# A hybrid decoder layer on one core: the FFN up-projection by Strassen's products, and the stages behind the retention issued in program order

## The chip, the core and the metric

One core of a Trainium2 chip runs the whole layer. The time of a run is the device time of that core in microseconds (us), from the program's start to its end; a profiled execution also gives its span (first to last recorded instruction) and the times of every instruction. TensorE (PE) multiplies, VectorE (DVE), ScalarE (ACT) and GpSimd (POOL) do the elementwise work, and the DMA engines move data between DRAM and the on-chip memory (SBUF). Matrix products land in PSUM.

## The reference, cut to what matters

Sequence of 16 meta tokens and 1024 tokens, width 1024, float32. The change touches what follows the retention: its output projection, the output projection of the differential attention, the gated merge with `w_out`, and the gated MLP.

```python
ro = (jax.nn.silu(rg) * ro) @ w_ret_o            # 4 heads x 512 -> 1024
do = do @ w_diff_o                               # 1024 -> 1024
mix = (sigmoid(g_ret) * ro + sigmoid(g_diff) * do) @ w_out
h = h + mix
u = rmsnorm(h, norm2_w)
up = causal_dwconv(u @ w_up, conv_w, conv_b)     # w_up: 1024 -> 2 x 2816, three taps
a, b = jnp.split(up, 2, axis=-1)
h = h + (jax.nn.silu(a) * b) @ w_down            # 2816 -> 1024
```

## The kernel before

Everything lies with channels on the 128 partitions and tokens along the free axis, 1040 tokens in three groups `QG` of 342, 342 and 342 columns (1026 of them are used behind the attention). Every float32 operand is split into a rounded high part and the rest, and a product is three matmuls, high by high, high by low, low by high (`bulk`, line 175 is the one place where they are recorded). A block of weights is 128 output channels by 1024 input channels, eight 128x128 tiles: `load_w` brings it in two halves of 128x512, ACT casts the high part (L227, tile `wh`), POOL subtracts for the low part (L230, tile `wl`). `next_w` keeps one block ahead.

The order on each engine comes from a scheduler that runs ahead over the whole program, bound by the buffers of the pools. Behind the retention come:

- `ret_out(h)`, the retention's output blocks, woven between the chunks of the next head; that of the last head stands alone at the end of `phase2`.
- `phase3`: the heads of the attention are reloaded and scaled (L986), eight output blocks of `w_diff_o` (three groups, 72 matmuls each), the gates from spilled tiles (sigmoid L996, multiplied on POOL L1006), the merge (L1012, L1013), its split (L242, L247), eight blocks of `w_out`, and the residual with its squares (L1034, L1040, L1041).
- `normed(m)`: the residual is scaled by the norm's weight and split (L250, L253); the sum of squares gives the reciprocal root `rb2` by a chain of some ten DVE operations (`rsqrt`, L273 to L293), and it is multiplied into the product only behind the matmul, where the up-projection leaves PSUM (L1094).
- `phase4`: for each of 22 f, two blocks of `w_up` (f and 22+f), 2 x 72 matmuls of 342 columns; each is scaled (L1094), convolved (`conv`, three DVE operations of 1024 columns, L1101 and L1103), silu on ACT (L1139), the product (L1140), its split by ACT (L242) and POOL (L247). Every two f, `down` adds 8 x 2 x 6 matmuls of 512 columns to the residual (L1118).

Of the kernel before, what the change touches and what calls it, by code (L numbers as in the profile page):

```python
# [97 lines left out]
class Builder:  # L98
    ATT_WEIGHT, RET_WEIGHT = 38.666666666666664, 27.0

    def __init__(self, ctx, tc, a, chunk_dec):
# [211 lines left out]
    def setup(self):  # L313
# [7 lines left out]
        pc = cp.tile([P, a["cols"].shape[1]], F32, name="cols")  # L321
# [7 lines left out]
    def constants(self):  # L329
# [8 lines left out]
        cr = cp.tile([P, nr], F32R, name="constsr")  # L338
# [405 lines left out]
    def phase1(self):  # L744
# [17 lines left out]
        order = []  # L762
        for n in range(0, NF, 2):
            down = [a["w_down"][n - 2], a["w_down"][n - 1]] if n else []
            up = [a["w_up"][f] for f in (n, NF + n, n + 1, NF + n + 1)]
            order += up[:2] + down + up[2:] if n < NF - 2 else up + down
        order += [a["w_down"][NF - 2], a["w_down"][NF - 1]]
# [193 lines left out]
    def phase2(self, rest, nrest):  # L961
# [12 lines left out]

    def phase3(self):
        V, A, G, S = self.V, self.A, self.G, self.S
        q = slice(HALO, T)
        dh, dl = [], []
        for h in range(DH):
            sp, sy = self.spill["do", h]  # L980
            d, y = self.big(), self.big()
            S.dma_start(out=d[:, q], in_=sp[:, q])
            for p, n in enumerate((258, 256, 256, 256)):
                t0 = HALO if p == 0 else NMETA + 256 * p
                S.dma_start(out=y[:, t0:t0 + n], in_=sy[p:p + 1, :n].to_broadcast([P, n]))
# [219 lines left out]
```

## Time and profile before

| | |
|---|---|
| three runs | 2597.95, 2599.13, 2600.05 us, median 2599.13 |
| profiled execution | 2597.52 us, its span 2595.7 us |
| PE busy | 97% of the span |
| DVE, ACT, POOL busy | 61%, 35%, 33% |
| PE's granted clock, mean | 0.99 |

The profiled execution is 1.8 us longer than its span; the difference lies around the span. A busy share is an average over the whole span. Matmul starts are recorded; one matmul's end overlaps the start of the next, so what a matmul costs is read from start to start.

### The profile page before, as it was taken

How to read it: one execution, taken by the hardware profiler on the slowest of the kernel's cores; microseconds unless marked ns; L12 is line 12 of the kernel's file. 1: busy time of each engine (PE TensorE's matmuls, PEld its weight loads, DVE VectorE, ACT ScalarE, POOL GpSimd, SP SyncE). 2: the span in 40 equal slices, each digit the busy share in tenths (PEclk: the TensorE clock that was granted, in tenths of full speed). 3: DMA queues.
4: the chain of work that ended last, by engine and by line, in shares of the span. 5: the costliest groups of instructions: out<-in, count | busy, mean ns of one | idle time of the engine just before them, and what ended most of it. 6: DMA issues, size and time to landing. Idle time of an engine off the chain costs nothing.

```text
span 2595.7 us, 40469 instructions
## 1 busy us (share of the span) xinstructions
PE 2518.1 (97%) x15444; PEld 2420.7 (93%) x15444; DVE 1575.6 (61%) x3239; ACT 899.0 (35%) x1879; POOL 852.7 (33%) x668
## 2 busy tenths in 40 slices
PE   7899999999999999999999998999999999999999
PEld 6888999999999999999999898999999999999998
DVE  8676756556473646453777888352466555555555
ACT  3244434344342434243456654332311111111111
POOL 4433343223132222212333332444333333332332
PEclk8999999999999999999999999999999999999999
DMA  4423141424233141423443434523111111111112
GB/s 176 103 70 101 54 130 62 125 82 117 81 81 102 61 117 58 125 84 109 112 107 89 114 91 130 167 94 110 46 49 45 45 49 49 48 43 49 49 49 85
DMA packets 171538, 224.55 MB, mean 87 GB/s; under 512 B 26712, under 2 KB 109264, under 8 KB 171344
## 3 DMA queue, kind: packets, MB, share of 16 engines
q1 hardware_dynamic: 165440, 202.70, 25.7%
q0 software_dynamic: 5760, 19.17, 3.6%
q8 instruction: 121, 1.98, 0.3%
q14 instruction: 73, 0.60, 0.1%
q10 hardware_dynamic: 144, 0.10, 0.0%
HBM read 160.20 MB, written 42.35 MB: 78 GB/s over the span
## 4 chain that ended last, share of the span: by engine, by line
PE 82%; DVE 9%; issue 4%; ACT 2%; DMA 2%; POOL 1%; SPq 1%; DVEq 0%; POOLq 0%; ACTq 0%
PE acc L175 47%; PE sc L175 27%; PE ot L175 3%; PE st L175 1%; PE sc L640 1%; DVE b L499 1%; ACT b L624 1%; DVE b L501 1%; DVE sh L498 1%; DVE b L617 1%; DVE b L247 1%; DMA b<-d 1%; DVE b L253 1%; DVE sql L247 1%; POOL wl L230 1%
## 5 line engine op out<-in xcount | busy, mean ns | idle before, releaser
L175 PE MATMUL acc<-b,wh 128*128 128x342 f32 (+3 forms) x6076 | 1485.0, 327 | 31.3 <-ACT wh L227 7.2
L175 PEld LDWEIGHTS acc<-b,wh 128*128 128x128 f32 x6076 | 1055.4, 190 | 46.5 <-ACT wh L227 7.1
L175 PE MATMUL acc<-b,wl 128*128 128x342 f32 (+3 forms) x3038 | 986.8, 325 | 0.8 <-POOL wl L230 0.8
L230 POOL TENSOR_TENSOR wl<-wr,wh 128x512 fp32r<-128x512 f32 x370 | 516.3, 1414 | 1081.3 <-ACT wh L227 1067.7
L175 PE MATMUL sc<-b,wh 128*128 128x342 f32 (+2 forms) x2452 | 616.9, 335 | 0.0
L175 PEld LDWEIGHTS acc<-b,wl 128*128 128x128 f32 x3038 | 576.4, 190 | 6.6 <-POOL wl L230 1.4
L175 PEld LDWEIGHTS sc<-b,wh 128*128 128x128 f32 x2452 | 432.7, 189 | 19.9
L227 ACT CAST wh<-wr 128x512 fp32r<-128x512 f32 x370 | 215.0, 618 | 583.8 <-issue 297.3
L175 PE MATMUL sc<-b,wl 128*128 128x342 f32 (+2 forms) x1226 | 409.7, 334 | 0.8 <-POOL wl L230 0.8
L247 POOL TENSOR_TENSOR b<-b,b 128x512 fp32r<-128x512 f32 (+2 forms) x90 | 147.3, 1637 | 317.5 <-ACT b L242 294.1
L175 PEld LDWEIGHTS sc<-b,wl 128*128 128x128 f32 x1226 | 231.7, 189 | 11.3 <-POOL wl L230 1.3
L242 ACT CAST b<-b 128x512 fp32r<-128x512 f32 (+2 forms) x135 | 100.1, 745 | 235.0 <-DVE b L1140 146.1
L624 ACT ACTIVATE b<-b,sm 128x272 f32<-128x272 f32 (+7 forms) x128 | 100.9, 788 | 187.7 <-DVE sm L623 159.7
L534 DVE TENSOR_TENSOR ev<-acc,b 128x342 f32<-128x342 f32 (+1 forms) x144 | 74.1, 515 | 151.1 <-PE acc L175 133.6
L1103 DVE SCALAR_TENSOR_TENSOR b<-b,cols,b 128x1024 f32<-128x1024 f32 x88 | 148.4, 1686 | 2.3
L617 DVE CUSTOM_DVE_ANT_0 b<-sc,consts 128x144 f32<-128x144 f32 (+6 forms) x224 | 106.0, 503 | 54.7 <-PE sc L175 54.6
L1094 DVE TENSOR_TENSOR b<-sc,b 128x342 f32<-128x342 f32 x84 | 42.5, 511 | 138.6 <-PE sc L175 138.6
L1118 DVE TENSOR_TENSOR b<-b,sc 128x512 f32<-128x512 f32 x117 | 78.6, 682 | 47.6 <-PE sc L175 47.6
L247 DVE TENSOR_TENSOR al<-sc,ah 128x512 fp32r<-128x512 f32 (+2 forms) x144 | 77.4, 539 | 47.0 <-ACT ah L242 44.9
L242 ACT CAST ah<-sc 128x512 fp32r<-128x512 f32 (+2 forms) x144 | 67.2, 468 | 110.4 <-PE sc L640 84.4
L500 POOL TENSOR_TENSOR sh<-sh,b 128x346 f32<-128x346 f32 (+1 forms) x48 | 48.9, 1019 | 143.2 <-DVE sh L498 120.5
L175 PE MATMUL sc<-b,b 128*128 128x264 f32 (+9 forms) x480 | 91.1, 310 | 1.4 <-DVE sm L617 1.4
(233 smaller groups left out, 2740.7 us busy)
## 6 DMA issues: line engine op xcount, KB each, us to landing
wr<-w_in SPq DMA_DIRECT2D x176, 256.0 KB
wr<-w_up SPq DMA_DIRECT2D x88, 256.0 KB
d<-ev SPq DMA_DIRECT2D x120, 171.0 KB
b<-b POOLq DMA_DIRECT2D x72, 260.0 KB, 4.3
b<-d SPq DMA_DIRECT2D x256, 64.0 KB
b<-d SPq DMA_DIRECT2D x24, 513.0 KB
wr<-w_down SPq DMA_DIRECT2D x44, 256.0 KB
b<-d SPq DMA_DIRECT2D x32, 260.0 KB
```

Of the source, the lines that this page charges most:

```text
L175: self.E.matmul(out, lhsT=l, rhs=r, start=start, stop=stop)
L227: self.A.copy(h, raw)
L230: self.G.tensor_sub(l, raw, h.bitcast(F32))
L242: self.A.copy(dh, src)
L247: (self.V if el == "V" else self.G).tensor_sub(dl, src, dh.bitcast(F32))
L500: G.tensor_mul(sh[:, :n], sh[:, :n], self.Sn[:, cs])
L534: V.tensor_mul(o[:, :n], ps[:, :n], self.rb[:, cs])
L617: V.tensor_tensor_reduce(out=sc_[:m, a0:a0 + sz], in0=ps[:m, :sz], in1=mk, scale=1.0, scalar=3e38, op0=ALU.add, op1=ALU.min, accum_out=sm[ ...
L624: A.activation(sc_[:m, :n], sc_[:m, :n], AF.Exp, bias=mx, scale=-1.0, accum_out=sm[:m, 10 + c:11 + c])
L1094: self.V.tensor_mul(up[:, t0:t0 + n], ps[:, :n], self.rb2[:, t0:t0 + n])
L1103: V.scalar_tensor_tensor(out=o[:, q], in0=up[:, NMETA - 2 + i:T - 2 + i], scalar=self.cw(i, fi), in1=o[:, q], op0=ALU.mult, op1=ALU.add)
L1118: self.V.tensor_add(h, h, ps)
```

## The change

The up-projection is cut into quarters: rows of `w_up` into lower and upper input channels (4 tiles each), its columns into the block of f and that of 22+f, the tokens into two halves of 516. The four quarter results come from seven products of quarter size (Strassen's algorithm in Winograd's form, called A, B, E, F, G, H, D), each 4 tiles x 3 matmuls x 2 pieces of 258 columns. Seven sums of token halves (`operand_a` to `operand_h`) are made once, seven weights for each f: two by DMAs that add while they write (`quad_sums`, on POOL's queue), two by POOL additions (S and T in `weights`), and all seven are split by ACT and POOL (`split_w`). The results are combined where they leave PSUM, the tap sums run in `act_steps` between the products of the next f, and every f's result goes to DRAM. `down` runs behind the last f and reloads them. The norm is now multiplied into the tokens before the products (`scaled`), so that sums can be formed.

`w_out` runs in two token halves, so its weights are loaded and split twice, and the norm of the first half runs in the second. From `back` on, the order on each engine is the program's own. `back` closes the pools of the first stages and opens new ones: `w2` with 128x512 quarters, PSUM as three double banks and two single ones. The last head's blocks 4 to 7 of `ret_out` move into `phase3`. The stages before are as they were, but for eight small memsets.

```diff
+        self.flush()
+        self.front.close()
...
+        self.wp = pool("w2", 11)
+        self.ps = pool("ps2", 3, space=PSUM)
+        self.queue = [a["w_ret_o"][14], a["w_ret_o"][15]] + [a["w_diff_o"][i] for i in range(8)] + 2 * [a["w_out"][i] for i in range(8)]
...
+        for i in (4, 2, 0):
+            self.coming.append(raws[i:i + 2])
+            self.fetch(self.queue.pop(0), raws[i:i + 2])
+        self.ready.append([self.split_w(r) for r in self.coming.pop(0)])
...
+    def split_w(self, raw):
+        w = self.quarter()
+        self.A.copy(w[0], raw)
+        self.G.tensor_sub(w[1], raw, w[0].bitcast(F32))
+        return w
...
+    def block(self, level=1):
+        w = self.ready.pop(0)
+        while len(self.ready) < level and self.coming:
+            self.arrive()
+            self.request()
+        return lambda k: tuple(t[:, k % 4, :] for t in w[k // 4])
...
+    def dbl(self): return self.ps.tile([P, 1024], F32, tag="d", name=self.nm("d"), bufs=3)
+    def sng(self): return self.ps.tile([P, 512], F32, tag="s", name=self.nm("s"), bufs=2)
...
+    HALF = [[(12, 256), (268, 256)], [(524, 258), (782, 258)]]
+    PIECES = [(0, 258), (258, 258)]
...
+        self.heads, self.wq, self.raws = [], {}, {}
+        nxt = self.normed_head(0)
+        for m in range(4, 8):
+            if m % 2 == 0:
+                w = self.block(m // 2 - 1)
+            outs, reads = self.triple()
+            self.product(outs, [(w(4 * (m % 2) + e), (self.gh[3][e], self.gl[3][e])) for e in range(4)])
+            for cs, p in reads:
+                V.tensor_add(self.like(self.racc[m], cs), self.like(self.racc[m], cs), p)
+            nxt()
+            nxt = self.normed_head(m - 3)
...
+            self.split(mh[m][:, 12:], ml[m][:, 12:], mx[:, 12:], el="G" if m % 2 and m < 7 else "V")
...
+        def finish(m, i, ps):
+            t0, n = self.HALF[i][0]
+            o = self.two(self.h[m][:, t0:t0 + 2 * n])
+            V.tensor_add(o, o, self.pair(ps, n))
+            hs = slice(8 + 516 * i, 524 + 516 * i)
+            S.dma_start(out=self.hs[m][:, 516 * i:516 * i + 516], in_=self.h[m][:, hs])
...
+                (V if i else G).tensor_add(sq[:, hs], sq[:, hs], x)
...
+            while m < 8:
+                w = self.block(2 - i)
+                ps = self.dbl()
...
+                finish(m, i, ps)
+                if i:
+                    if m == 0:
+                        squares(0)
+                    elif m == 1:
+                        stat()
+                    elif m == 2:
+                        spread(0)
+                    elif m < 7:
+                        for k in (2 * (m - 3), 2 * (m - 3) + 1):
+                            self.operand_a(k)
+                    if 3 <= m < 6:
+                        self.pre_weights(m - 3)
+                    if 2 <= m < 5:
+                        self.pre_loads(m - 2)
+                    elif m == 5:
+                        self.quad_loads(0)
+                    elif m == 6:
+                        self.quad_sums(0)
+                m += 1
+        squares(1)
+        self.weights(0, "SE")
+        self.quad_loads(1)
+        self.pro = {}
+        self.first_t(0)
+        self.first_t(1)
+        self.quad_sums(1)
+        stat()
+        self.first_t(2)
+        self.weights(0, "F")
+        self.first_b(0)
+        spread(1)
+        self.weights(1, "SE")
+        self.first_b(1)
+        self.first_b(2)
...
+    def scaled(self, k, i):
+        x = self.h[k][:, 8 + 516 * i:524 + 516 * i]
+        self.V.scalar_tensor_tensor(out=x, in0=x, scalar=self.n2[k], in1=self.rb2[:, 8 + 516 * i:524 + 516 * i], op0=ALU.mult, op1=ALU.mult)
...
+    def operand_a(self, k):
+        self.put("A" if k < 4 else "B", k % 4, self.scaled(k, 0))
...
+    def operand_e(self):
+        for k in range(4):
+            self.scaled(k, 1)
+            self.V.tensor_sub(self.half(k, 0), self.half(k, 0), self.half(k, 1))
+            self.put("E", k, self.half(k, 0), "G" if k % 2 else "V")
...
+    def operand_f(self):
+        for k in range(4):
+            self.scaled(4 + k, 1)
...
+    def operand_h(self):
+        for k in range(4):
+            self.V.tensor_sub(self.half(k, 1), self.half(k, 1), self.half(4 + k, 1))
+            self.put("H", k, self.half(k, 1), "G" if k % 2 else "V")
...
+    def operand_d(self):
+        for k in range(4):
+            self.put("D", k, self.half(4 + k, 1), "G")
...
+    def quad_loads(self, f):
+        blk, blk2 = self.a["w_up"][f], self.a["w_up"][NF + f]
+        lo, hi = slice(0, 4), slice(4, 8)
+        s1, s3 = self.raw_quarter(blk2[:, lo, :]), self.raw_quarter(blk2[:, lo, :])
+        ra = self.raw_quarter(blk[:, lo, :])
+        rb = self.raw_quarter(blk[:, hi, :])
+        rd = self.raw_quarter(blk2[:, hi, :])
+        self.raws[f] = dict(a=ra, b=rb, d=rd, s1=s1, s3=s3)
+    def quad_sums(self, f):
+        r = self.raws[f]
+        self.nc.gpsimd.dma_start(out=r["s1"], in_=self.a["w_up"][NF + f][:, 4:, :], accum_op=ALU.add)
+        self.nc.gpsimd.dma_start(out=r["s3"], in_=self.a["w_up"][f][:, :4, :], accum_op=ALU.add)
...
+    def weights(self, f, names):
+        q, r = self.wq.setdefault(f, {}), self.raws[f]
+        for n in names:
+            if n == "S":
+                self.G.tensor_add(r["a"], r["a"], r["s1"])
+            elif n == "T":
+                self.G.tensor_add(r["b"], r["b"], r["a"])
+            else:
+                q[n] = self.split_w(r[dict(A="a", B="b", F="a", H="s3", E="s1", G="d", D="b")[n]])
...
+    def quad_product(self, ps, f, name, more=False):
+        w = self.wq[f].pop(name)
+        outs = [(ps[:, 512 * g:512 * g + 512], t0, n) for g, (t0, n) in enumerate(self.PIECES)]
+        self.product(outs, [((w[0][:, k, :], w[1][:, k, :]), self.xs(name, k)) for k in range(4)], not more, True, more)
...
+        def taps(o, fi, up, cs):
+            for i in (1, 0):
+                V.scalar_tensor_tensor(out=o[:, cs], in0=up[:, at(cs, i)], scalar=self.cw(i, fi), in1=o[:, cs], op0=ALU.mult, op1=ALU.add)
...
+        first(oa, f, ua)
...
         for f in range(NF):
+            todo = {1: ["F", "H", "TG", "D"], 2: ["SE", "F", "H", "TG", "D"]}.get(f + 1, ["A", "SF", "B", "H", "E", "TG", "D"])
...
+                for n in next(steps, ""):
+                    self.weights(f + 1, n)
...
+            pw = self.dbl()
+            self.quad_product(pw, f, "F")
             if f == 0:
-                pg = self.kouter([self.next_w(), self.next_w()], lambda k: self.vh2[k], lambda k: self.vl2[k], QG)
-                self.flush()
-                y = []
-                for i in range(2):
-                    up = self.big()
-                    for (t0, n), ps in zip(QG, pg[i]):
-                        V.tensor_mul(up[:, t0:t0 + n], ps[:, :n], self.rb2[:, t0:t0 + n])
-                    y.append(self.conv(i * NF, up))
-                ya, yb = y
+                self.operand_h()
+            V.tensor_sub(bd(sw), bd(st), self.pair(pw, 258))
+            others()
+            if f >= self.PRO:
+                self.quad_product(pt, f, "B", True)
+                A.copy(bd(ua[:, :516]), self.pair(pt, 258))
...
+            if f == 0:
+                self.weights(0, "G")
+            self.quad_product(pw, f, "H", True)
+            if f == 0:
+                self.operand_g()
+            V.tensor_sub(bd(su), self.pair(pw, 258), bd(st))
+            others()
...
+            if f in pvs:
+                pv = pvs.pop(f)
             else:
-                ya, yb = self.up(f), self.up(NF + f)
-            A.activation(ya[:, q], ya[:, q], AF.Silu)
-            V.tensor_mul(ya[:, q], ya[:, q], yb[:, q])
-            a, b = self.big(F32R), self.big(F32R)
-            self.split(a[:, q], b[:, q], ya[:, q], el="G")
-            gh.append(a)
-            gl.append(b)
-            if prev and (f == NF - 1 or f % 2 == 0 and f < NF - 2):
-                self.down(*prev, False)
...
-        self.down(*prev, True)
+                pv = self.dbl()
+                self.quad_product(pv, f, "E")
+            V.tensor_sub(bd(ub[:, 516:1032]), bd(su), self.pair(pv, 258))
...
+            if f == 0:
+                self.weights(0, "TD")
+            self.quad_product(pw, f, "G", True)
+            if f == 0:
+                self.operand_d()
+            V.tensor_sub(bd(ub[:, :516]), self.pair(pw, 258), bd(st))
+            for _ in act:
+                pass
+            others()
+            act = self.act_steps(f, ua, ub)
+            next(act)
+            self.quad_product(pv, f, "D", True)
+            V.tensor_add(bd(ua[:, 516:1032]), bd(sw), self.pair(pv, 258))
+            for _ in range(2):
+                next(act)
+            for s in steps:
+                for n in s:
+                    self.weights(f + 1, n)
+            if f + 2 < NF:
+                self.quad_sums(f + 2)
+            if last:
+                down = self.down_split()
...
+    def down_split(self):
...
+            self.split(gh[-1], gl[-1], x[:, :SEQ], el="G")
...
-    b.phase3()
-    b.phase4()
+    with tc.manual_schedule():
+        b.back(ctx)
+        b.phase3()
+        b.phase4()```

What stands in the rows of three queues, at three places:

SyncE's queue (SP) at the end of the retention, where it issues loads. L221 (before), L224 and L1008 (after) load halves of weight blocks into `wr`, L982 and L985 (before) and L1072 (after) load the attention's spilled heads; in brackets are the semaphores waited for. Of before, where the halves stand between the heads:

```order
L985 DMA b_18547<-d_6981 128x256 [waits DMAHW2_49]
L982 DMA b_18558<-d_8523 128x1026 [waits DMAHW3_49,PE_49]
L221 DMA wr_18316<-w_ret_o 128x512 [waits DMAHW4_49,Pool_49]
L221 DMA wr_18406<-w_diff_o 128x512 [waits DMAHW5_49,Pool_49]
L985 DMA b_18559<-d_8524 128x258 [waits DMAHW6_49,PE_49]
L985 DMA b_18559<-d_8524 128x256 [waits DMAHW7_49]
```

Of the changed kernel, where the first stages end (L224) and `back` begins (L1008):

```order
L819 DMA vl_17893<-d_11424 128x128 [waits DMAHW5_49]
L224 DMA wr_18125<-w_ret_o 128x512 [waits DMAHW6_49,Pool_49]
L1008 DMA wr_18330<-w_ret_o 128x512 [waits DMAHW3_49,DMAHW2_49,DMAHW4_49,DMAHW1_49,DMAHW5_49,DMAHW0_49,DMAHW6_49,DVE_49,DMAHW7_49,PE_49,Pool_49]
L1008 DMA wr_18331<-w_ret_o 128x512
L1008 DMA wr_18328<-w_ret_o 128x512
L1008 DMA wr_18329<-w_ret_o 128x512
L1008 DMA wr_18326<-w_diff_o 128x512
L1008 DMA wr_18327<-w_diff_o 128x512
L1072 DMA b_18346<-d_1095 128x1026
```

Three loads of two halves now stand in a row, and the first waits for PE, DVE, POOL and all eight queues of loads.

DVE's queue in the up-projection. Of before, one f: L1094 takes a product out of PSUM (`sc`, `acc`) times `rb2`, L1101 and L1103 are the taps, L1118 adds a product of `down`:

```order
L1094 TENSOR_TENSOR b_21313<-sc_21288,b_20233 128x342
L1094 TENSOR_TENSOR b_21313<-sc_21315,b_20233 128x342
L1094 TENSOR_TENSOR b_21313<-sc_21341,b_20233 128x342
L1101 TENSOR_SCALAR b_21367<-b_21313,cols 128x1024
L1118 TENSOR_TENSOR b_19411<-b_19411,sc_21387 128x512
L1103 SCALAR_TENSOR_TENSOR b_21367<-b_21313,cols,b_21367 128x1024
L1118 TENSOR_TENSOR b_19411<-b_19411,acc_21395 128x512
L1103 SCALAR_TENSOR_TENSOR b_21367<-b_21313,cols,b_21367 128x1024
L1118 TENSOR_TENSOR b_19413<-b_19413,acc_21403 128x512
L1140 TENSOR_TENSOR b_21274<-b_21274,b_21367 128x1024
```

Of the changed kernel, f = 0: L1307 and L1302 are the sums of `operand_h` and `operand_g`, L250 the low parts (two of four, POOL has the others), L1451 and L1466 take the products F and H out of PSUM (`d_20901`):

```order
L1307 TENSOR_TENSOR b_19474<-b_19474,b_19482 128x516
L250 TENSOR_TENSOR b_20928<-b_19474,b_20927 128x516
L1307 TENSOR_TENSOR b_19476<-b_19476,b_19484 128x516
L1307 TENSOR_TENSOR b_19478<-b_19478,b_19486 128x516
L250 TENSOR_TENSOR b_20930<-b_19478,b_20929 128x516
L1307 TENSOR_TENSOR b_19480<-b_19480,b_19488 128x516
L1451 TENSOR_TENSOR sw_20898<-u_20612,d_20901 128x516
L1302 TENSOR_TENSOR b_19482<-b_19482,b_19474 128x516
L250 TENSOR_TENSOR b_20977<-b_19482,b_20976 128x516
L1302 TENSOR_TENSOR b_19484<-b_19484,b_19476 128x516
```

Ahead of the products' results stand sums and splits of operands, where before only work on earlier results stood.

POOL's queue in the up-projection. Of before, f by f: two halves of each of two blocks, and the split of the gated product (L247):

```order
L230 TENSOR_TENSOR wl_22151<-wr_22152,wh_22150 128x512
L230 TENSOR_TENSOR wl_22151<-wr_22156,wh_22150 128x512
L230 TENSOR_TENSOR wl_22250<-wr_22251,wh_22249 128x512
L230 TENSOR_TENSOR wl_22250<-wr_22255,wh_22249 128x512
L247 TENSOR_TENSOR b_22246<-b_22146,b_22245 128x1024
```

Of the changed kernel, one f: L1335 and L1336 are the DMAs that add, L1343 and L1345 the additions S and T, L1003 the low parts in the order A, F, B, H, E, G, D:

```order
L1335 DMA wr_22302<-w_up 128x512
L1336 DMA wr_22304<-w_up 128x512
L1003 TENSOR_TENSOR wl_22446<-wr_22306,wh_22445 128x512
L1343 TENSOR_TENSOR wr_22306<-wr_22306,wr_22302 128x512
L1003 TENSOR_TENSOR wl_22482<-wr_22306,wh_22481 128x512
L1003 TENSOR_TENSOR wl_22512<-wr_22308,wh_22511 128x512
L1003 TENSOR_TENSOR wl_22542<-wr_22304,wh_22541 128x512
L1003 TENSOR_TENSOR wl_22585<-wr_22302,wh_22584 128x512
L1345 TENSOR_TENSOR wr_22308<-wr_22308,wr_22306 128x512
L1003 TENSOR_TENSOR wl_22615<-wr_22310,wh_22614 128x512
L1003 TENSOR_TENSOR wl_22654<-wr_22308,wh_22653 128x512
```

Four subtractions and one of twice the width have become nine and two DMAs.

## Rows read from the trace of the kernel before

**Rows 1.** The profile page: busy time of each engine (share of the span, instructions), and the chain of work that ended last, by engine.

```profile
PE 2518.1 (97%) x15444; PEld 2420.7 (93%) x15444; DVE 1575.6 (61%) x3239; ACT 899.0 (35%) x1879; POOL 852.7 (33%) x668
...
PE 82%; DVE 9%; issue 4%; ACT 2%; DMA 2%; POOL 1%; SPq 1%; DVEq 0%; POOLq 0%; ACTq 0%
```

**Rows 2.** Busy time by stretches of the span: `w_out`, the norm and the up-projection with `down`. Columns: length; PE, weight loads, DVE, ACT, POOL busy (instructions); PE's granted clock; share of the DMA engines; GB/s.

```profile
1700.00:1800.00 100.00, 99.11 (x628) 98.55 (x627) 42.70 (x55) 23.17 (x36) 35.46 (x26) 1.00 0.26 83
1800.00:1900.00 100.00, 99.80 (x631) 99.10 (x630) 45.61 (x54) 28.61 (x45) 39.35 (x34) 1.00 0.17 56
1900.00:2000.00 100.00, 100.00 (x562) 93.14 (x562) 61.95 (x67) 17.67 (x25) 35.10 (x22) 1.00 0.15 46
```

**Rows 3.** Timeline of PE and DVE at the end of the retention, matmuls of 342 columns: start, duration (up to the end of the last of the group), count, and in brackets the idle time ahead with what ended it.

```profile
1629.76 0.32 PE L175 MATMUL acc<-b,wl 128*128 128x342 f32 x1
...
1633.07 0.32 PE L175 MATMUL acc<-b,wl 128*128 128x342 f32 x1
...
1634.72 1.29 DVE L986 SCALAR_TENSOR_TENSOR b<-b,qkw,b 128x1026 f32<-128x1026 f32 x1 [4.56 <-DMA b<-d]
1635.92 0.92 DVE L957 TENSOR_TENSOR b<-b,acc 128x342 f32<-128x342 f32 x2
...
1636.48 0.94 PE L175 MATMUL acc<-b,wh 128*128 128x342 f32 x2 [3.10 <-DVE b L957]
1637.21 0.49 PE L175 MATMUL acc<-b,wl 128*128 128x342 f32 x1
...
1642.63 0.49 PE L175 MATMUL acc<-b,wh 128*128 128x342 f32 x2
```

**Rows 4.** Busy time of PE in the same stretch: length, busy (matmuls), granted clock, DMA share, GB/s.

```profile
1630.00:1633.00 3.00, 3.00 (x21) 1.00 0.51 178
...
1636.00:1640.00 4.00, 3.52 (x12) 0.50 0.02 8
...
1643.00:1646.00 3.00, 3.00 (x21) 1.00 0.79 215
```

**Rows 5.** Timeline of PE in the attention: matmuls of 256 columns that stand behind one another (four steps from the first to the last row of each place).

```profile
923.50 0.28 PE L175 MATMUL ot<-al,vh 128*128 128x256 f32 x1
...
923.97 0.28 PE L175 MATMUL ot<-ah,vl 128*128 128x256 f32 x1
...
926.44 0.28 PE L175 MATMUL ot<-al,vh 128*128 128x256 f32 x1
...
926.92 0.28 PE L175 MATMUL ot<-ah,vl 128*128 128x256 f32 x1
```

**Rows 6.** Groups of DVE's instructions from 1640 us to the end: line, operation, output and inputs, shape, count, busy us, mean ns, idle us ahead.

```profile
L1103 DVE SCALAR_TENSOR_TENSOR b<-b,cols,b 128x1024 f32<-128x1024 f32 x88 | 148.4, 1686 | 2.3
...
L1118 DVE TENSOR_TENSOR b<-b,sc 128x512 f32<-128x512 f32 x117 | 78.6, 682 | 47.6 <-PE sc L175 47.6
...
L1140 DVE TENSOR_TENSOR b<-b,b 128x1024 f32<-128x1024 f32 x22 | 26.8, 1219 | 1.3
...
L986 DVE SCALAR_TENSOR_TENSOR b<-b,qkw,b 128x1026 f32<-128x1026 f32 x2 | 2.6, 1281 | 0.0
...
L279 DVE TENSOR_TENSOR sq<-sq,ry 128x342 f32<-128x342 f32 x2 | 1.0, 516 | 0.1
```

**Rows 7.** The same for ACT.

```profile
L227 ACT CAST wh<-wr 128x512 fp32r<-128x512 f32 x166 | 95.0, 618 | 387.0 <-issue 191.5 <-PE sc L175 108.0 <-PE acc L175 84.5
...
L242 ACT CAST b<-b 128x1024 fp32r<-128x1024 f32 x22 | 23.1, 1050 | 146.1 <-DVE b L1140 146.1
...
L457 ACT COPY b<-ot 128x342 f32<-128x342 f32 x3 | 1.3, 442 | 4.9 <-PE ot L175 4.9
...
L250 ACT ACTIVATE ryh<-ry 128x342 fp32r<-128x342 f32 x1 | 0.5, 491 | 6.7 <-DVE ry L283 6.7
```

**Rows 8.** Timeline of POOL while it splits two weight halves with no DVE operation on SBUF alone beside it.

```profile
1653.34 2.55 POOL L230 TENSOR_TENSOR wl<-wr,wh 128x512 fp32r<-128x512 f32 x2 [10.06 <-ACT wh L227]
...
1655.84 2.41 POOL L247 TENSOR_TENSOR b<-b,b 128x1026 fp32r<-128x1026 f32 x1
```

**Rows 9.** Timeline of the first 9 us: the first loads, the first matmul, and DVE beside POOL.

```profile
1.19 0.89 SPq L221 DMA_DIRECT2D wr<-w_in  x2
...
6.27 0.75 DVE L252 TENSOR_SCALAR b<-b,cols 128x1040 fp32r<-128x1040 f32 x1
6.42 1.27 ACT L227 CAST wh<-wr 128x512 fp32r<-128x512 f32 x2 [3.74 <-DMA wr<-w_in]
7.06 1.30 DVE L253 SCALAR_TENSOR_TENSOR b<-b,cols,b 128x1040 fp32r<-128x1040 f32 x1
7.11 2.38 POOL L230 TENSOR_TENSOR wl<-wr,wh 128x512 fp32r<-128x512 f32 x1 [6.67 <-DMA wr<-w_in]
...
7.17 0.63 PE L175 MATMUL acc<-b,wh 128*128 128x348 f32 x1 [7.17 <-ACT wh L227]
```

**Rows 10.** Timeline in the up-projection: POOL splits two weight halves while DVE runs three taps.

```profile
1951.94 1.88 DVE L1101 TENSOR_SCALAR b<-b,cols 128x1024 f32<-128x1024 f32 x1
1951.97 2.99 POOL L230 TENSOR_TENSOR wl<-wr,wh 128x512 fp32r<-128x512 f32 x2 [8.91 <-ACT wh L227]
1953.85 3.51 DVE L1103 SCALAR_TENSOR_TENSOR b<-b,cols,b 128x1024 f32<-128x1024 f32 x2
```

**Rows 11.** The page's DMA issues on POOL's queue: output and input, queue, count, KB each, median us from issue to landing.

```profile
b<-b POOLq DMA_DIRECT2D x72, 260.0 KB, 4.3
```

More of the change, by code (lines that the diff above doesn't have):

```diff
@@ L761, in phase1 @@
         seq += fill[7 * DH:]
[L762 to L767, printed above, removed]
         self.loaded = []
-        self.stream = ([a["w_in"][b] for _, _, b in seq] + [a["w_ret_o"][i] for i in range(16)]
-                       + [a["w_diff_o"][i] for i in range(8)] + [a["w_out"][i] for i in range(8)] + order)
+        self.stream = [a["w_in"][b] for _, _, b in seq] + [a["w_ret_o"][i] for i in range(14)]
         self.norm_in()
@@ new lines, in work, with pair, two, product @@
+    def work(self):
+        return self.tp.tile([P, 1032], F32, tag="work", name=self.nm("u"), bufs=3)
+    def dbl(self): return self.ps.tile([P, 1024], F32, tag="d", name=self.nm("d"), bufs=3)
+    def sng(self): return self.ps.tile([P, 512], F32, tag="s", name=self.nm("s"), bufs=2)
+    @staticmethod
+    def pair(ps, n):
+        return ps.rearrange("p (a b) -> p a b", a=2)[:, :, :n]
+    @staticmethod
+    def two(t): return t.rearrange("p (a b) -> p a b", a=2)
+    def product(self, outs, pairs, start=True, stop=True, more=False):
+        last = len(pairs) - 1
+        for i, ((wh, wl), (xh, xl)) in enumerate(pairs):
+            for l, x, f, e in ((wh, xh, start and i == 0, False), (wh, xl, False, False), (wl, xh, False, stop and i == last)):
+                for o, t0, n in outs:
+                    self.E.matmul(o[:, :n], lhsT=l, rhs=x[:, t0:t0 + n], start=f, stop=e, skip_group_check=more)
@@ new lines, in triple, with like @@
+    def triple(self):
+        d, s = self.dbl(), self.sng()
+        banks = [d[:, :512], d[:, 512:], s]
+        outs = [(o, t0, n) for o, (t0, n) in zip(banks, QG)]
+        reads = [(slice(14, 698), self.pair(d, 342)), (slice(698, 1040), s[:, :342])]
+        return outs, reads
+    @staticmethod
+    def like(t, cs):
+        v = t[:, cs]
+        return v.rearrange("p (a b) -> p a b", a=2) if cs.stop - cs.start == 684 else v
+    HALF = [[(12, 256), (268, 256)], [(524, 258), (782, 258)]]
@@ new lines, in phase4 @@
+        h = done
+        for p in range(NF // 2):
+            gh, gl = down
+            last = p == NF // 2 - 1
+            for m in range(8):
+                if m % 4 == 0:
+                    w = self.block()
+                next(act, None)
+                if m == (6 if p == NF // 2 - 2 else 0) and not last:
+                    self.down_fetch(p + 1)
+                o = 2 * (m % 4)
+                ps = self.dbl()
+                self.product([(ps[:, :512], 0, 512), (ps[:, 512:], 512, 512)], [(w(o + i), (gh[i], gl[i])) for i in range(2)])
+                for cs in [slice(0, 512), slice(512, SEQ)] if last else [slice(0, SEQ)]:
+                    V.tensor_add(h[m][:, cs], h[m][:, cs], ps[:, cs])
+                    if last:
+                        self.S.dma_start(out=self.a["out"][m][:, cs], in_=h[m][:, cs])
+                if m == (7 if p == NF // 2 - 2 else 2) and not last:
+                    down = self.down_split()
```

390 lines of the change are left out of this document (256 added, 134 removed).

## The prediction

> **What bounds the kernel now.** I read the busy times and the chain first, then the stretches, then PE's timeline, then what the other engines do in the stretch that changes. PE is busy 97% of the span and holds 82% of the chain [rows 1]; in the up-projection it is busy all of each 100 us at the full clock, while DVE has 62, ACT 18 and POOL 35 [rows 2]. So this part costs what its matmuls cost. From start to start, 21 matmuls of 342 columns took 1633.07 - 1629.76 = 3.31 us, 0.1576 each [rows 3]. At a granted clock of 0.50, 1.2 of 2.4 GHz, the 19 from 1637.21 to 1642.63 took 5.42 us, 0.285 each [rows 3, 4], behind an idle stretch of 3.1 us. PE stood there for DVE's L957, which stood behind the scaling of a head (L986) that waited 4.56 us for its load [rows 3].
>
> **What the change saves on PE.** Before, 44 blocks x 72 = 3168 matmuls of 342 columns: 3168 x 0.1576 = 499.3 us. After, 22 x 7 x 24 = 3696 of 258 columns. The trace has none of 258; those of 256 take (0.47 + 0.48)/8 = 0.119 [rows 5]. In proportion 258 take 0.120: 443.5 us. That is 55.8 less. `w_out` in halves has 384 matmuls of 256 and 384 of 258 for 576 of 342: 45.7 + 46.1 - 90.8 = 1.0 more. `down`, the attention's output and the stages ahead keep their columns. Two things of before also go: the stop at 1633 (3.1 idle, and 0.285 - 0.1576 = 0.127 x 21 = 2.7 by the clock [rows 3, 4]), and 0.9 + 0.2 in `w_out` and the norm [rows 2]: 6.9. Ceiling of the gain: 55.8 - 1.0 + 6.9 = 61.7 us. Whether it comes depends on who has the operands ready.
>
> **The price list.** By lines through the rows nearest: DVE with two inputs in SBUF 0.516 at 342 columns, 1.219 at 1024, so 0.70 at 516; with a scalar 1.281 at 1026, so 0.71 [rows 6]. POOL takes 2.55/2 = 1.28 for a weight half and 2.41 for 1026 [rows 8], so 1.30 at 516. ACT 0.62 for 512, 1.05 for 1024 [rows 7]. DVE out of PSUM 0.68 at 512 [rows 6].
>
> **DVE and POOL take turns.** At 7.06 a DVE operation with two SBUF inputs starts and runs its 1.30 us; POOL's subtraction of 0.05 later takes 2.38, which is the wait to 8.36 plus 1.13 [rows 9]. In the up-projection three taps that alone take 0.75 (nearest, 1040 columns) + 2 x 1.28 = 3.3, and 2.55 of POOL's, 5.9 together, lasted from 1951.94 to 1957.36, 5.4 us [rows 6, 8 to 10]: 0.92 of the sum, far from 3.3 side by side. The Trainium skill, "SBUF — State Buffer", section "Who interferes with whom", says that a DVE instruction with two SBUF inputs contends with a GpSimd instruction that reads SBUF. By its exclusive lock held for whole instructions the start's stop below would be 29.7 us, by the rows' 0.92 it is 26; I take the rows. In what follows I call work of this kind turns, add it up over both engines, and multiply by 0.92.
>
> **The costs, in order of the program.**
> 1. *The closed pools.* The first load of `back` waits for PE, DVE and POOL, where before the halves were issued among other loads. So PE stands for issue, landing, cast and handoff: the first load of the program was issued at 1.19 and its cast began at 6.42, PE at 7.17 [rows 9], 6.0 us behind 520 KB of others; 260 KB on POOL's queue land in 4.3 [rows 11]. Landing 4.0, cast 0.6, the rest 0.3: 4.9, with 2.7 of half clock 7.6. I take 7.5; bounds 5 (landing 3, less clock) and 10.
> 2. *`w_diff_o`.* PE needs 72 x 0.1576 = 11.3 us for a block, the turns per block are about 8. The heads are now reloaded behind the weights, two stages ahead of their use, so the wait of 4.56 is mostly hidden. Handoffs at their reloads, a PSUM bank that `merge(0)` still reads, and a split behind a POOL product remain, each an estimate of one or two operations of the price list: 1.4, 1.2 and 1.4, so 4. Bounds 2 and 6.
> 3. *The second half of `w_out`.* For m = 3 to 5 a loop has PE work of 48 x 0.12 = 5.7 us. Its turns: POOL four subtractions (the next block, and `pre_weights`), 5.1; DVE the squares' sum and two of `scaled` with split, 0.7 + 2 x 1.4 = 3.5. 8.6 x 0.92 = 7.9, so 2.2 x 3, and 0.8 at `spread(0)`: 7.5. Bounds 5 and 12. Before, the norm came after the matmul (L1094) and asked for nothing here.
> 4. *The start of the products.* From the last `w_out` matmul the second half's norm takes: add 0.7, square 0.5, sum 0.7, split 1.3, the matmuls 0.6, the root 6.7 (so long ACT waited for it [rows 7]), split 0.9, spread and two copies 1.4, eight handoffs of 0.1: 13.6. Then turns for all operands of that half: E and F 9.6 each (four `scaled`, four sums, two low parts on DVE and two on POOL), H and G 6.8 each, D 5.2, 38.0; eight weight operations 10.3. 48.3 x 0.92 = 44.4, so D is ready at 58. PE's work until then is A, B three times, E twice, F, H, G: 11 x 24 x 0.12 = 31.7, and 0.5. 58.0 - 32.2 = 25.8; I take 26. DVE's rows show the order: L1451, which frees F's PSUM, stands behind all of `operand_h`. Bounds 25 and 30 with turns, 7.3 without (rival below).
> 5. *f = 1 and 2* have no B between F and H to cover the subtraction; taps stand ahead of it: 4. Bounds 0 and 9.
> 6. *Steady f.* PE 168 x 0.12 = 20.2. Turns: POOL nine operations, 11.6; DVE eight taps of 512 columns at 0.70 and two products at 0.62, 6.8; 18.4 x 0.92 = 16.9. Hidden: 0; it costs from 20.2 on. The accumulating DMAs have 512 KB a f; the page has 4.3 us [rows 11], POOL's row has two issues and one subtraction ahead of the addition that needs them.
> 7. *To `down`.* The first split of `down` stands on ACT behind the last taps' first step, which waits for D. Cast 1.05, POOL 2.41 a piece [rows 7, 8]: the second low part comes at 0.8 + 1.2 + 1.05 + 2 x 2.41 = 8 us, PE has 4 x 0.46 of matmuls until then: 6. Before, `down` of the pair before covered it. Bounds 4 and 8.
>
> Sum: 7.5 + 4 + 7.5 + 26 + 4 + 0 + 6 = 55. Net: -61.7 + 55 = -6.7. On the profiled execution's 2597.5 this gives **2590.8 us**; the profiled execution lies 1.6 under the median of the three runs, within their spread, so I add nothing. I predict 2591.
>
> **The rivals.**
> *A: the steady part is bound by the turns.* For: nothing but their sum is 1.8 us (18.4) to 3.3 (16.9) under PE's 20.2; POOL must besides issue two DMAs and wait for the first: 4.3 - 1.3 of its own work leaves up to 3 us, in which DVE has turns to take only if its taps happen to be due. If 2.9 us of that are lost, f takes 18.4 + 2.9 = 21.3, 1.1 x 19 = 21 more: 2612, slower. It decides from 20.2 + 6.7/19 = 20.6 us per f. Against: DVE has 6.8 us of turns to place, and weights are asked for a whole f ahead. Chance 0.28.
> *B: the turns cost little at the start.* If DVE (22.4) and POOL (25.9) of the 48.3 ran side by side, D would be ready at 13.6 + 25.9 = 39.5, the stop 7.3 for 26, and the second half of `w_out` would not wait (5.1 under 5.7): 26 less, 2565. For: the queues are ordered so that low parts alternate between the two. Against it is that the two waited for one another wherever both had work [rows 9, 10]. A part of it is enough for a time between. Chance 0.22.
> *The forecast*, 0.50, by its own bounds 2577 to 2608.
>
> **Numbers.** 0.2%, about what a measurement of this kernel can tell, is 5.2 us: same is 2594 to 2604 against the median. Of the forecast's 0.50 I give 0.27 to faster, 0.16 to same, 0.07 to slower; B's 0.22 is faster; of A's 0.28 0.02 is same, 0.26 slower. Faster 0.49, same 0.18, slower 0.33. Range: half of B lies under 2564, a third of A over 2618, so 2563 to 2618 leaves out 0.2.
>
> **What will show it.** PE's starts in the products 0.119 to 0.121 apart; an idle PE of 4 to 6 us near 1635 ended by a load's cast; gaps from the last `w_out` matmul to D of f = 0 of 26 us in sum, ended by ACT or DVE at operands H, G, D; f = 3 to 21 at 20.2 us each without waits (A: waits at F, A or G for weights on POOL); 6 us ahead of `down`. It is wrong if f takes over 20.5 us, if the start's gaps are under 15, or if 258 columns take more than 0.122.

## The result, and the profile after

The changed kernel takes 2618.82 us (median of 4 runs, 2613.93 to 2621.89), the kernel before 2598.54 (4 runs, 2596.12 to 2600.05): 1.0077 of the time before, 95% interval 1.0059 to 1.0095. It is slower; 2591 was forecast. The profiled execution took 2621.89, its span 2620.1.

The page of after, beside [rows 1]: PE is busy 15.5 us less, POOL 227.5 more, ACT 133 more.

```profile
PE 2502.6 (96%) x16168; PEld 2395.0 (91%) x16168; DVE 1586.0 (61%) x3222; ACT 1031.9 (39%) x2108; POOL 1080.2 (41%) x847
```

The stretches, beside [rows 2]: the end of `w_out`, the start of the products, f = 1 to 3, and steady f.

```profile
1800.00:1862.00 62.00, 53.49 (x399) 52.03 (x399) 28.34 (x41) 20.68 (x38) 29.72 (x23) 0.92 0.42 124
1862.00:1926.00 64.00, 48.70 (x303) 46.01 (x303) 37.68 (x50) 23.57 (x42) 34.93 (x26) 0.79 0.20 54
1926.00:1985.00 59.00, 50.70 (x384) 49.83 (x383) 43.98 (x45) 24.48 (x37) 39.85 (x31) 0.91 0.42 103
2100.00:2200.00 100.00, 98.16 (x805) 97.09 (x804) 68.87 (x74) 42.91 (x68) 68.81 (x52) 1.00 0.43 114
```

PE is full in none of these stretches; its mean granted clock is 0.92, 0.79 and 0.91 in the first three and 1.00 in the last. What PE waited for most from 1900 to 2400 us (total, times, longest):

```profile
PE d L1049 <- DVE sw L1451: 12.8, 19, 3.3
PE d L1049 <- ACT b L245: 11.3, 4, 4.3
```

By the starts of the first matmul of each stage (a stage named after products ends where the next product starts), against matmuls at 0.1198 a piece of 258 columns, 0.157 of 342 and 0.23 of 512:

| stage | after, us | matmuls alone | lost | forecast |
|---|---|---|---|---|
| closed pools: 1628.6 to 1632.3 from start to start, and the clock | | | 6.1 | 7.5 |
| `w_diff_o` | 98.2 | 90.3 | 7.8 | 4 |
| second half of `w_out` | 61.4 | 46.0 | 15.4 | 7.5 |
| start, A to D of f = 0 | 63.4 | 34.5 | 28.9 | 26 |
| f = 1, 2 | 35.2 | 25.9 | 9.3 | 4 |
| f = 3, 4 | 47.9 | 40.2 | 7.7 | 0 |
| f = 5 to 20 | 334.4 | 322.0 | 12.4 | 0 |
| f = 21 and the first pair of `down` | 50.6 | 42.3 | 8.2 | 6 |

That is 96 us against 55. An f in which PE waits for nothing takes 20.27 us (run 2), 0.1207 a piece, so 2.3 of the 12.4 and 0.3 of the 7.7 are the matmuls' own. A loss holds idle time and slower matmuls. At the start 91 of the 288 pieces came some 0.21 apart, at a mean granted clock of 0.79; that is 8.6 of the 28.9 us, and 20 gaps make the rest. In the second half of `w_out` it is 4.2 of 15.4. No run here changes the clock alone, so what a full clock would give back is not shown.

From `ret4`, the first matmul behind the closed pools, to the last matmul of all it is 983.1 us; this stretch compares the kernels below, since it began between 1625.9 and 1632.5 us in the traces of the changed kernel and its variants, although the code ahead of it is the same.

### The profile page after: what moved, and what is told of

Same layout as the page of the kernel before. It is cut to its first block, busy times and chain, and to the rows that moved or that the text cites. A ratio compares the mean times of both kernels' runs of the same rounds, so it can differ in the third digit from the quotient of the medians.

```text
span 2620.1 us, 42810 instructions
## 1 busy us (share of the span) xinstructions
PE 2502.6 (96%) x16168; PEld 2395.0 (91%) x16168; DVE 1586.0 (61%) x3222; ACT 1031.9 (39%) x2108; POOL 1080.2 (41%) x847
## 5 line engine op out<-in xcount | busy, mean ns | idle before, releaser
L178 PE MATMUL acc<-b,wh 128*128 128x342 f32 (+2 forms) x4784 | 1164.9, 326 | 20.6 <-ACT wh L230 6.0
L178 PEld LDWEIGHTS acc<-b,wh 128*128 128x128 f32 x4784 | 831.1, 191 | 24.5 <-DVE b L256 6.0
L1049 PE MATMUL d<-b,wh 128*128 128x258 f32 (+3 forms) x4000 | 768.2, 311 | 46.9 <-ACT b L245 14.2
L178 PE MATMUL acc<-b,wl 128*128 128x342 f32 (+2 forms) x2392 | 773.2, 323 | 0.0
L1049 PEld LDWEIGHTS d<-b,wh 128*128 128x128 f32 x4000 | 612.5, 194 | 87.5 <-ACT b L245 16.1
L233 POOL TENSOR_TENSOR wl<-wr,wh 128x512 fp32r<-128x512 f32 x202 | 277.6, 1389 | 635.4 <-ACT wh L230 629.2
L1049 PE MATMUL d<-b,wl 128*128 128x258 f32 (+3 forms) x2000 | 456.9, 310 | 7.2 <-POOL wl L1003 7.2
L1003 POOL TENSOR_TENSOR wl<-wr,wh 128x512 fp32r<-128x512 f32 x250 | 364.2, 1473 | 233.8 <-ACT wh L1002 202.9
L1049 PEld LDWEIGHTS d<-b,wl 128*128 128x128 f32 x2000 | 332.7, 194 | 23.4 <-POOL wl L1003 8.1
L250 POOL TENSOR_TENSOR b<-b,b 128x512 fp32r<-128x512 f32 (+4 forms) x105 | 173.8, 1662 | 249.2 <-ACT b L245 212.7
L1002 ACT CAST wh<-wr 128x512 fp32r<-128x512 f32 x250 | 143.9, 616 | 295.1 <-POOL wr L1343 143.3
L230 ACT CAST wh<-wr 128x512 fp32r<-128x512 f32 x202 | 119.0, 618 | 198.4 <-issue 105.9
L1380 DVE SCALAR_TENSOR_TENSOR b<-b,cols,b 128x512 f32<-128x512 f32 x164 | 191.0, 1185 | 2.9
L1517 DVE TENSOR_TENSOR b<-b,d 128x1024 f32<-128x1024 f32 (+1 forms) x96 | 108.0, 1132 | 133.4 <-PE d L1049 133.4
L245 ACT CAST b<-b 128x512 fp32r<-128x512 f32 (+4 forms) x164 | 116.3, 720 | 179.7 <-DVE b L1121 45.8
L245 ACT CAST ah<-sc 128x512 fp32r<-128x512 f32 (+2 forms) x144 | 67.2, 467 | 112.2 <-PE sc L643 88.0
L250 DVE TENSOR_TENSOR al<-sc,ah 128x512 fp32r<-128x512 f32 (+2 forms) x144 | 77.4, 539 | 46.9 <-ACT ah L245 45.0
```

What stands on the lines that cost most here:

```text
L178: self.E.matmul(out, lhsT=l, rhs=r, start=start, stop=stop)
L230: self.A.copy(h, raw)
L233: self.G.tensor_sub(l, raw, h.bitcast(F32))
L245: self.A.copy(dh, src)
L250: (self.V if el == "V" else self.G).tensor_sub(dl, src, dh.bitcast(F32))
L1002: self.A.copy(w[0], raw)
```

## The experiments

Each run changes the changed kernel. Runs 1 to 6 are one execution each. Lengths are from the starts of matmuls, as in the table: A0 is the first product A of f = 0, and "A0 to D0" has both products in it.

**1. The taps' step of f = 5 to 20.** In after six taps (L1380) stand ahead of L1451, which frees F's PSUM for H. DVE's timeline, two f (start, duration):

```profile
2163.61 0.68 DVE L1451 TENSOR_TENSOR sw<-b,d 128x516 f32<-128x516 f32 x1
...
2176.84 7.76 DVE L1380 SCALAR_TENSOR_TENSOR b<-b,cols,b 128x512 f32<-128x512 f32 x6
2184.53 0.68 DVE L1451 TENSOR_TENSOR sw<-b,d 128x516 f32<-128x516 f32 x1
```

They run on until L1451 begins, so DVE has no idle time ahead of it; f takes 2184.53 - 2163.61 = 20.92. PE's first matmul of H waits for it, here behind the first of the two:

```profile
2164.35 0.75 PE L1049 MATMUL d<-b,wh 128*128 128x258 f32 x4 [0.38 <-DVE sw L1451]
```

The edit:

```diff
-            def others():
-                next(act, None)
+            def others(step=True):
+                if step:
+                    next(act, None)
...
-                others()
+                others(False)
```

> The taps' step between A and F of the next f is left out, so that on DVE four instead of six taps of the f before stand ahead of the subtraction L1451 that frees F's PSUM for H. Theory (order on DVE's queue: six taps, stretched by POOL's turns to 7.8 us, end after F does): the wait of H on L1451, 0.37 us and 0.55 with the restart in each f from 5 on, goes; f takes 20.3 us instead of 20.9, and the whole is about 10 us shorter, a span near 2610. Rival (the turns of DVE and POOL as a whole bind the steady part): the wait moves to another product of the same f, and f stays at 20.7 to 20.9.

```profile
2180.93 2.98 DVE L1380 SCALAR_TENSOR_TENSOR b<-b,cols,b 128x512 f32<-128x512 f32 x4
2186.20 0.69 DVE L1452 TENSOR_TENSOR sw<-b,d 128x516 f32<-128x516 f32 x1 [2.28 <-PE d L1049]
```

DVE now waits 2.28 us for F (the subtraction is L1452 here). f = 5 to 20 took 324.3 for 334.4, 20.27 each. The theory held. The stretch took 967.3 for 983.1, more than the 10 expected: 3.2 more came at f = 4 and 1.9 at f = 1 and 2. f = 3 kept its 24.3.

**2. The same wait from the other side.** The order stays, POOL's work goes.

```diff
+            elif f >= 3 and n != "A":
+                w = self.wp.tile([P, 4, P], F32R, tag="wh", name=self.nm("wh"))
+                self.A.copy(w, r[...])
+                q[n] = (w, self.one_low)
```

> Leaves out part of the computation: for f = 3 to 21 POOL makes one low part of the weights, A's, and the other six products read it, so that POOL's turns per f fall from 11.6 to 3.9 us; every other instruction stays. Theory (six taps in DVE's row end late because they share turns with POOL): alone they take 6 x 0.7 = 4.3 us, end before F does, and H no longer waits for L1451; f takes 20.3 us for 20.9 although the order of DVE's row is unchanged. Rival (DVE's row by its own length): the taps stay near 7 us and the wait stays.

```profile
2180.39 5.34 DVE L1386 SCALAR_TENSOR_TENSOR b<-b,cols,b 128x512 f32<-128x512 f32 x6
2185.66 0.69 DVE L1457 TENSOR_TENSOR sw<-b,d 128x516 f32<-128x516 f32 x1
```

The six taps take 5.34 for 7.76 (4.3 were expected), PE waits for nothing from 1960 to 2330 us, f = 5 to 20 takes 324.3. So the wait needs both: six taps in the queue ahead, and POOL's work that stretches them by 2.4 us. In after two subtractions and the issue of the two adding DMAs lie beside the six taps, here one subtraction; which of these stretches them is not told apart. Either remedy is enough for f = 5 to 20. f = 3 and 4 took 40.5 for 47.9, so the 4.0 us that f = 3 kept in run 1 come from POOL's work too.

**3. The second half of `w_out`.** In after, ACT's casts of the next block (L1002) stand behind those of `operand_a` (L245), and these wait for DVE and through it for the block before:

```profile
1831.54 0.62 ACT L245 CAST b<-b 128x516 fp32r<-128x516 f32 x1 [1.43 <-DVE b L1280]
1832.07 2.17 ACT L1002 CAST wh<-wr 128x512 fp32r<-128x512 f32 x4
...
1832.76 5.87 POOL L1003 TENSOR_TENSOR wl<-wr,wh 128x512 fp32r<-128x512 f32 x4 [7.51 <-ACT wh L1002]
...
1833.77 0.74 PE L1049 MATMUL d<-b,wh 128*128 128x258 f32 x4 [1.42 <-ACT wh L1002]
...
1836.99 0.80 PE L1049 MATMUL d<-b,wl 128*128 128x258 f32 x2 [2.48 <-POOL wl L1003]
```

POOL had been idle for 7.5 us: a full row of turns would not leave that.

```diff
-                w = self.block(2 - i)
+                w = self.block(2)
```

> In the second half of w_out the weights are split two blocks ahead instead of one. Theory (a chain in ACT's queue: the casts of the next block stand behind the squares and casts that wait for the block before): the waits of PE on wh L1002 (1.4 us twice) and wl L1003 (2.5 us twice, 0.3) go, the half takes 48 us instead of 61.4 from its first matmul to A, 10 to 14 us less. Rival (the sum of DVE's and POOL's turns, 7.9 us a loop against 5.75 of PE): the splits come earlier but the same work is done, so PE waits as long a loop or two later, or the start is later by as much; less than 4 us in all.

The half took 49.4 us for 61.4, as the theory has it. But the products A and B, 19.7 from A0 to E0 in after, took 26.6: PE waits 3.8 us at the norm's statistics for ACT. The whole stretch gained 8.6. The next run moves what stands in the way there:

```diff
-                    elif m < 7:
+                    elif m < 6:
...
         squares(1)
+        self.operand_a(6)
+        self.operand_a(7)
```

> On top of weights split two blocks ahead, the last two of operand_a (k = 6, 7) stand behind the last block's residual and squares instead of ahead of them. Theory (with PE no longer late, DVE's row puts two scalings and splits, some 5 us, between the last w_out product and its norm, and the norm's end decides when E can begin): A to E1 falls from 40.9 to about 35 us, the kernel is 14 us shorter from the last blocks of the retention to the end than the changed kernel, against 8.6 with the two blocks alone. Rival (the sum of the elementwise work from the second half of w_out to D is what counts): the time moves on to F, H and G and the whole gains less than 2 us over the two blocks alone.

A to E1 took 37.7 us, 3.2 less than the 40.9, where 6 less was expected; the stretch 972.0, 11.1 less than in after. That is 2.5 more than with the two blocks alone, where the theory has 5.4 and the rival less than 2: between the two, nearer to the rival.

**4. What binds the start.** In after the first low part of E waits for a cast that stands on ACT behind B's copy, and each later one of DVE's for its own cast:

```profile
1880.82 0.59 ACT L1364 COPY u<-d 128x516 f32<-128x516 f32 x1 [2.30 <-PE d L1049]
1881.30 0.62 ACT L245 CAST b<-b 128x516 fp32r<-128x516 f32 x1
1881.96 0.70 DVE L250 TENSOR_TENSOR b<-b,b 128x516 fp32r<-128x516 f32 x1 [2.85 <-ACT b L245]
...
1884.79 1.79 POOL L250 TENSOR_TENSOR b<-b,b 128x516 fp32r<-128x516 f32 x1 [6.24 <-ACT b L245]
...
1886.14 1.00 DVE L250 TENSOR_TENSOR b<-b,b 128x516 fp32r<-128x516 f32 x1 [0.69 <-ACT b L245]
```

Three runs change who makes the low parts of E, F, G and H; E0 to D0 took 43.8 us in after, and 43.8 to 44.0 in the runs above, which leave it as it is. The edits are shown for E; F, G and H are changed alike. All on DVE:

```diff
-            self.put("E", k, self.half(k, 0), "G" if k % 2 else "V")
+            self.put("E", k, self.half(k, 0))
```

> At the start all low parts of the sums E, F, G and H are made on DVE (0.70 us each) instead of half of them on POOL (1.30). Theory of the prediction (turns add up): the sum of turns falls by 8 x 0.6 = 4.8 us and D of f = 0 ends 4 to 5 us earlier. Rival (DVE's own row of instructions binds, with a wait of 0.69 us for ACT's cast ahead of each low part): DVE gets 8 x (0.70 + 0.69) more, some of it hidden, and D ends 5 to 10 us later.

48.6 us, 4.8 longer: against the turns, whose sum fell, and near the rival's 5. All on POOL:

```diff
-            self.put("E", k, self.half(k, 0), "G" if k % 2 else "V")
+            self.put("E", k, self.half(k, 0), "G")
```

> The counterpart of the run with all low parts on DVE: at the start POOL makes all low parts of E, F, G and H. Theory (DVE's own row binds the start: for each low part that it makes it waits 0.69 us for ACT's cast and works 0.70): DVE loses 8 x 1.4 us of its row, and from A0 to D0 the start takes 4 to 8 us less than the 63.4 of the changed kernel. Rival (turns add up): their sum rises by 8 x 0.6 = 4.8 us and the start is that much longer.

42.6 us, 1.1 shorter (63.4 to 62.3 from A0 to D0): the sum rose by 4.8 and the time didn't, but 4 to 8 did not come either, and at A of f = 3 nothing of it was left (98.7 from A0, 98.6 in after). And POOL's half left out:

```diff
+        if name in "EFGH" and k % 2:
+            self.A.copy(h[:, c], x)
+        else:
+            self.split(h[:, c], l[:, c], x, el=el)
```

> Leaves out part of the computation: of the sums E, F, G and H the low parts of k = 1 and 3, POOL's, are not made, and the products read that of the k before. DVE's row and ACT's casts stay as they are, POOL has 8 x 1.30 us less at the start. Theory of the prediction (turns of DVE and POOL add up there): E0 to D0 takes 8 to 10 us less than the 43.8 of the changed kernel. Rival (the chain of DVE's own row, which waits 0.69 us for a cast ahead of each low part and for PE's results, binds; POOL only stretches some operations): 2 to 4 us less.

39.3 us, 4.4 shorter: half of what turns would give, a little over the rival's 2 to 4. What DVE waited for at the start, in after (first row, 1862 to 1926) and in this run (second, 1861 to 1921), total, times and longest:

```profile
DVE b L250 <- ACT b L245: 8.8, 9, 2.9
```

```profile
DVE b L250 <- ACT b L245: 8.8, 9, 2.9
```

The nine waits for casts are the same to a tenth, though POOL has less to do. With all low parts on POOL one of them is left:

```profile
DVE b L250 <- ACT b L245: 0.7, 1, 0.7
```

There 8.1 us of waits and 8 x 0.7 us of work went from DVE's row, and the start gained 1.1. So the start is not the sum of the turns, and it is not DVE's row alone. That a chain through DVE's sums, ACT's casts and the low parts of whichever engine has them holds it fits all three runs, but it is argued and not shown.

**5. L1451 and L1466 ahead of the operands.** DVE's rows in the order printed ahead suggested it:

```diff
+            V.tensor_sub(bd(sw), bd(st), self.pair(pw, 258))
             if f == 0:
                 self.operand_h()
-            V.tensor_sub(bd(sw), bd(st), self.pair(pw, 258))
```

> For f = 0 the subtractions that free F's and H's PSUM (L1451, L1466) stand ahead of the operands of H and G on DVE instead of behind them. Theory (the start is bound by the elementwise chain that ends in D's low parts): F, H and G of f = 0 spread differently, but D ends where it did, within 1 us. Rival (the two subtractions' place holds PE, as rows of DVE's queue suggest): H starts 4 us earlier, G as well, and D ends 4 to 7 us earlier.

E0 to D0 took 49.0 us, 5.3 more: both were wrong. DVE now stands idle until F is done and begins with H's operand only then, and the same for H and G (the subtractions are L1449 and L1464 here):

```profile
1895.01 0.69 DVE L1449 TENSOR_TENSOR sw<-u,d 128x516 f32<-128x516 f32 x1 [3.03 <-PE d L1049]
...
1904.80 0.70 DVE L1464 TENSOR_TENSOR su<-d,u 128x516 f32<-128x516 f32 x1 [3.34 <-PE d L1049]
```

Their place behind the operands was right.

**6. D's low parts, and the first pair of `down`.**

```diff
-            self.put("D", k, self.half(4 + k, 1), "G")
+            self.put("D", k, self.half(4 + k, 1))
...
-            if last:
-                down = self.down_split()
...
             if last:
+                down = self.down_split()
                 self.arrive()
```

> Two places far apart. The low parts of operand D are made on DVE, which is idle then, instead of four in a row on POOL: D of f = 0 (6.4 us for 2.9 of matmuls, two waits for POOL) takes 4 us or less, 3 to 4 saved. And the first pair of down is fetched, cast and split before the last E instead of behind D's result: the waits of 3.3 and 1.8 us at the first product of down and the half clock behind them go, 7 us saved between D21 and the second pair. Rival for the second (the low parts on POOL and the weights of down are late in any case): a wait of 3 us or more for weights stays.

D took 6.1 for 6.4, and E0 to D0 43.5: missed, since D's casts come in after T on ACT and DVE shares turns with POOL's weights. `down` gained 4.0 of 7: PE stands 2.2 us for a weight's low part, which now comes behind the split on POOL; a wait for weights stays, as the rival has it, but under its 3 us.

**7. Together.**

> The edits of place and order together: the taps' step behind L1451, w_out's weights split two blocks ahead with the last operands behind the norm, the weights of w_diff_o two ahead and its last four heads scaled one product earlier, the copy of the last B behind operand E, for f = 0 and 1 the taps behind the next L1451, and the first pair of down fetched ahead of the residual and split, behind its weights, before the last E. Theory (what the change lost is waits made by the order in the queues): the parts add, 10 us in f = 5 to 20, 5 before, 11 in w_out and A to B, 5 in w_diff_o, 6 at down: from the last retention blocks to the end 946 us for 983, about 2582 in all, 0.6% faster than the kernel before. Rival (DVE's and POOL's sums bind, and what is saved in one place is waited for in the next): 960 or more, no faster than before.

2594.85 us, 0.9988 of before (0.9979 to 0.9997); the stretch 957.2, nearer to the rival's 960 than to the 946 of the theory. `w_diff_o` gained nothing (98.2), and six casts in a row behind the last merge stopped `w_out` for 2.9 us at its head; its first half took 52.0 for 45.2. With POOL's low parts besides it was 0.9996 (0.9986 to 1.0005), A0 to A3 2.4 us longer (theory: within 2; rival: 3 or more). Without the two edits in `w_diff_o`, and with the weights of f = 3 cast earlier:

```diff
-            todo = {1: [...], 2: ["SE", "F", "H", "TG", "D"]}
+            todo = {1: [...], 2: ["SE", "F", "H", "TG", "D"], 3: ["AS", "FB", "HE", "TGD"]}
```

> The edits together without the two in w_diff_o (they gained nothing there, and three blocks of w_out were split in a row behind the last merge: 6.8 us of PE's time at the start of w_out), and with the weights of f = 3 cast ahead of D of f = 2, so that A's copy of f = 3 does not stand on ACT behind a cast that waits for POOL's T. Theory (waits made by the order in the queues): 957 - 7 - 4 = 946 us from the last retention blocks to the end, about 2585 in all, 0.5% faster than the kernel before. Rival (the elementwise sums bind): the 4 us at f = 3 come back at the next f, 951 or more.

**2587.21 us, 0.9964 of before (0.9951 to 0.9976)**, the stretch 953.0. Steady f is full, and `down` starts without a wait:

```profile
2100.00:2200.00 100.00, 100.00 (x831) 100.00 (x830) 64.81 (x75) 44.02 (x70) 72.36 (x56) 1.00 0.46 118
```

f = 3 and 4 gained 0.4 of the 4 us expected (PE still waits 4.5 us for A's copy at f = 3), and the stretch is over the rival's 951, so the rival was right on that.

## Why the prediction was wrong

- **What PE saves** was right: 258 columns take 0.1207 in an f without a wait, where 0.120 was forecast, 2.6 us less over all 3696. POOL's adding DMAs, 5.3 us to landing for 4.3 [rows 11], made POOL wait some 2 us in each f of after; no wait of PE is put down to them.
- **Step 6, steady f, failed.** "Hidden: 0" compared a sum of turns with PE's time over a whole f. The sum does fit: with the order changed f takes 20.27 (run 1). What it can't show is one queue at one place: six taps and L1451 have to fit between D's result and the end of B, 7.9 us. They take 5.0 by the price list, 5.34 + 0.69 = 6.0 beside little of POOL's work (run 2) and 7.76 + 0.68 = 8.4 in after. f took 20.90 for 20.2: 12.4 us, of which either remedy took off 10.1. f = 3 and 4 lost 7.7 more, 3.2 of it at f = 4 to the same order (run 1) and 4.0 at f = 3, where A's copy stands on ACT behind a cast that waits for POOL; run 2 took both away. The 20.1 are half of the 41 us that the costs were too low. Rival A named the steady part as slow, but not this cause, and put it at 1.1 us an f where 0.78 came.
- **Step 3 was mis-sized**, 15.4 for 7.5, and for a wrong reason: not turns, but ACT's order (run 3), which took 12.0 off the half, though only 8.6 off the whole.
- **Step 4 was near in size by luck**, 28.9 for 26, and its mechanism was wrong: of the runs on the low parts the sum of turns had the sign wrong twice and the size wrong by two once (run 4). It has no term for the clock, and 8.6 of the 28.9 are matmuls at the lower clock. What binds there instead stays open. The 13.6 us for the norm held in sum: `w_out` ended at 1862.3, DVE's first `scaled` of the second half began at 1875.7.
- **Step 5** was 9.3 for 4: H waited for L1451 3.3 us at f = 1 and 1.9 at f = 2, G 0.9 for L1466, and from 1926 to 1945 the granted clock was 0.80 to 0.84.
- **Steps 1, 2 and 7** were 6.1, 7.8 and 8.2 for 7.5, 4 and 6. In step 2 the heads' reloads and low parts, thought mostly hidden, stopped PE four times within the first two blocks, 4.2 us; what would hide them was not found (run 7). Step 7's mechanism held: PE waited 3.3 and 1.8 us for the splits, and with the pair fetched and split earlier 8.0 of the 8.2 went (run 7).
- **Rival B** did not come: POOL and DVE do wait for one another. The rule of the Trainium skill, "SBUF — State Buffer", section "Who interferes with whom", stands: six taps take 5.34 us beside little POOL work and 7.76 beside more, so the two contend. Its use as a sum over a stage was the fault.

`w_diff_o` began 6.4 us earlier than in before (1657.5 for 1663.9), though the stop that goes (5.8) and step 1 (6.1) nearly cancel. From 1580 to 1625 us PE waited 7.3 us in before and 1.1 in after, probably since the heads' scalings and splits no longer stand in DVE's queue there; the prediction counted only the stop. This is most of the reason why the profiled execution missed the forecast by 31 us (2621.9 for 2590.8) and not by 41.

## What to carry to other kernels

Adding up engine time shows whether a stage can be hidden, not whether it is: for each product ask which instruction frees its operand or bank, what stands ahead of that instruction in the same queue, and what those wait for. Where an order is written by hand, one step too early on DVE or ACT costs PE in every round of a loop, and it is cheap to move. An algorithm that saves matmuls needs its operands ahead of PE; the start of such a stage, where nothing is ahead, can cost half of what the steady part saves.

## What was not expected

An instruction that frees a bank can stand too early: moved ahead of independent work, it made DVE wait 3.0 and 3.3 us for PE and cost 5.3 (run 5). What stays open is the 31 us that the start still loses with everything together (65.9 from A to D of f = 0, 34.5 of them matmuls at the full clock), and some 8 to 10 in `w_diff_o`: no edit tried here that keeps the whole computation shortened the start by more than 1.1, and none was seen to shorten `w_diff_o`.
